# Output projection of a hybrid attention layer on one Trainium2 core: column blocks 2 to 5 with six of 16 pairs of k tiles as 2x2 block products in seven parts

## The chip, the cores and the metric

The kernel runs on one NeuronCore of a Trainium2 chip. The core has a matrix engine (TensorE, PE in the profile, with PEld for its weight loads) and four others that work beside it: VectorE (DVE), ScalarE (ACT), GpSimd (POOL) and SyncE (SP), which here only issues transfers. Each runs its own list of instructions in order and waits on semaphores. PE writes to PSUM, eight banks of 128x512 floats; everything else lies in SBUF.

The metric is the time of one execution on the device, in microseconds (us). A profile is one execution taken by the hardware profiler.

## The reference

One layer with 256 frames and width 4096: an input projection, forgetting attention and an RWKV-7 recurrence side by side, a gate, and then the part that the change is about, the output projection with a residual layer norm:

```python
h = jnp.concatenate([fox_out, rwkv_out], axis=-1) * jax.nn.silu(z.astype(f32))
out = jnp.einsum('bsc,cd->bsd', h.astype(x.dtype), w_out)
x = _layernorm(ALPHA * x.astype(f32) + out.astype(f32), ln_gain, ln_bias, LN_EPS).astype(x.dtype)
```

`h` is 256x4096 and `w_out` 4096x4096, in float32.

## The kernel before

**Products.** Every float32 factor is split in two: `hi`, its rounding to the matrix engine's format (a CAST on ACT, L146), and `lo`, the rest (a TENSOR_TENSOR subtract on DVE, L147). A product of two factors is three matmuls that add up in one PSUM bank: h.hi, l.hi and h.lo, always in this order (L908 to L910). Each is 128x128 times 128x512.

**Tiling.** The 4096 rows of `w_out` are 32 k tiles of 128, taken in 16 pairs `q`; its columns are eight blocks `b` of 512 (`OB`); the 256 frames are two halves `m` of 128. For each block the loop goes over 16 jobs `(b, q)`. A job loads one raw tile of weights (128 x 1024, two k tiles, 512 KB, L226), splits it, and feeds four products (two k tiles, two halves), that is 12 matmuls. Blocks 0 and 1 come first and share the time with the end of the recurrence; their jobs 14 and 15 stand last, in the order (0,14), (0,15), (1,14), (1,15). Then blocks 2 to 7 follow one after the other.

**What sets the order of the weights.** `load` issues raw tiles on SP's queue into four buffers (tag `wr`); `fetch` splits the next one; `weights` keeps three split jobs ahead. There are four buffers for `hi` (tag `wh`) and three for `lo` (tag `wl`), so the `lo` of a job can only be written when PE has done with the `lo` of the job three places before it. A framework's scheduler then writes each engine's list; `issue_after` holds an instruction behind another one of that list.

**Behind each block.** `add` (L923, L924) adds ALPHA times the residual to the bank and takes the statistics for the norm, `gain` (L932) multiplies by the norm's gain, and for the first four blocks L935 and L936 split the second half once more for the end of the kernel. `load_tok(b)` (L887) brings the residual, the gain and two small rows `rr`, from which L899 and L900 make a row for the norm on DVE. The left factor `ht[k]` is a tile of 128 x 2 x 256 (hi and lo of both halves). GpSimd has nothing to do in blocks 2 to 7.

Of the kernel before, what the change touches and what calls it, by code (L numbers as in the profile page):

```python
# [47 lines left out]
HOLD = 46  # L48
W = {"fo": 7, "vs": 2, "np": 4, "gp": 5, "tp": 4, "d1": 8, "d2": 12, "xp": 3, "fs": 4, "fp": 5}
# [38 lines left out]
def layer(ctx: ExitStack, tc: tile.TileContext, xt, xtok, w_main, w_lora, w_first, muv, w_o, up, par, mulora, fbias, lng, lnb, cst, out):  # L88
# [125 lines left out]
    outs = [(b, q) for r in (range(CUT), range(CUT, KT // 2)) for b in range(2) for q in r] + [(b, q) for b in range(2, NB) for q in range(KT // 2)]  # L214
    stream += [(f"wo{b}_{q}", w_o[b][:, 2 * q : 2 * q + 2, :]) for b, q in outs]
# [4 lines left out]
    raws = []  # L220

    def load():
        if stream:
            name, src = stream.pop()
            raw = wpool.tile([P, 1024], F32, tag="wr", name=name, bufs=4)
            nc.sync.dma_start(out=raw, in_=src.rearrange("p k c -> p (k c)"))  # L226
            raws.append((name, raw))

    def fetch():
        while len(raws) < 3 and stream:  # L230
            load()
        if raws:
            name, raw = raws.pop(0)
            if name not in kept:
                ready.append((name, *split(raw, 1024, name)))
                return
            hl = []
            for j in range(4):
                hl.append(xpool.tile([P, OB], F32R, tag=f"x{4 * kept[name] + j}", name=f"{name}_{j}"))
            for j in range(2):  # L240
                r = raw[:, j * OB : (j + 1) * OB]
                nc.scalar.copy(hl[j], r)
                nc.vector.tensor_tensor(hl[2 + j], r, hl[j].bitcast(F32), ALU.subtract)
            ready.append((name, hl[:2], hl[2:]))

    def weights(name):
        while len(ready) < 3 and (stream or raws):
            fetch()
        got, hi, lo = ready.pop(0)
        assert got == name  # L250
        return hi, lo

    def block(n, b):
        if n == 0 and b == 0:
            return acc_0
        acc = [pp.tile([P, 512], F32, tag="pp", name=f"acc{n}_{b}_{m}") for m in range(2)]
        for q in range(KT // 2):
            hi, lo = weights(f"w{n}_{b}_{q}")
# [28 lines left out]
    def issue(out, src):  # L287
        tc.keep_in_program_order(nc.sync.dma_start(out=out, in_=src))
# [16 lines left out]
    lr = const.tile([LORA, 2, 2, S], F32R, name="lr")  # L305
# [596 lines left out]
    def part(t, j):  # L902
        return t[j] if isinstance(t, list) else t[:, j * OB : (j + 1) * OB]

    def project(acc, k, j, m, hi, lo):
        hi, lo = part(hi, j), part(lo, j)
        tt = slice(m * P, (m + 1) * P)
        nc.tensor.matmul(acc, ht[k][:, 0, tt], hi, start=(k == 0), stop=False)  # L908
        nc.tensor.matmul(acc, ht[k][:, 1, tt], hi, start=False, stop=False)  # L909
        nc.tensor.matmul(acc, ht[k][:, 0, tt], lo, start=False, stop=(k == KT - 1))  # L910
# [4 lines left out]
    sums = None  # L915

    def add(m, b):
# [5 lines left out]
        nc.vector.scalar_tensor_tensor(res[m][:, o], res[m][:, o], ALPHA, acc[m], ALU.mult, ALU.add)  # L923
        nc.vector.bn_stats(st[m][:, b, :], res[m][:, o])  # L924
# [5 lines left out]
    def gain(m, b):  # L930
        o = slice(b * OB, (b + 1) * OB)
        nc.vector.tensor_tensor(res[m][:, o], oacc[b][m] if m and b == NB - 1 else res[m][:, o], lgain[b], ALU.mult)  # L932
        if m and b < HALVED:
            gx[b] = [rpool.tile([P, OB], F32R, name=f"g{'hl'[j]}{b}") for j in range(2)]
            nc.scalar.copy(gx[b][0], res[m][:, o])  # L935
            nc.vector.tensor_tensor(gx[b][1], res[m][:, o], gx[b][0].bitcast(F32), ALU.subtract)  # L936

    gx = {}

# [38 lines left out]
    for b, q in outs:  # L978
        if q == 0:
            pool, tag = (ps, "ps") if b == 1 or b and b % 2 == 0 else (pp, "pp")  # L980
            oacc[b] = [pool.tile([P, 512], F32, tag=tag, name=f"oacc{b}_{m}") for m in range(2)]
        acc = oacc[b]
        hi, lo = weights(f"wo{b}_{q}")
        for j in range(2):
# [9 lines left out]
            elif b > 1 and k == (10 if b == 2 else 4):  # L994
                load_tok(b)
            elif (b, k) == (2, 20):
                own = rpool.tile([P, 2, OB], F32, name="own")
# [8 lines left out]
        if q < KT // 2 - 1:  # L1006
            continue
        if b == 0:
# [13 lines left out]
        if b < NB - 1:  # L1022
            with tc.issue_after(latest[0].ins):
                for m in range(2):
                    add(m, b)
                for m in range(2):
                    gain(m, b)
# [75 lines left out]
    folded = [rpool.tile([P, OB], F32R, name=f"f{'hl'[j]}") for j in range(2)]  # L1103
# [97 lines left out]
```

## Time and profile before

| | |
|---|---|
| Time, median of 3 runs | 1914.63 us (1914.19 to 1915.65) |
| The profiled execution: its time, its span | 1915.52 us, 1913.7 us |
| PE busy, DVE busy, ACT busy, POOL busy | 1902.5, 1399.2, 987.5, 261.1 us |
| Granted clock of TensorE, mean | 0.999 |
| Raw tiles of `w_out`: number, size, issue to landing | 128, 512 KB, 4.3 us |
| Stretch 1650 to 1700 us (blocks 2 and 3): PE, DVE, ACT, POOL busy | 50.00, 31.53, 23.78, 0.00 us |

The span is the profiled part of the execution; 1.8 us of the execution's time lie around it. Matmuls overlap in the records (0.39 us each, one begun every 0.23 us), so a busy PE is one that has no gap, not one at its peak. A group of instructions is shown by its line, its engine, output and input, with the number of them, busy time, mean, and then the idle time ahead of them and what ended it.

### The profile page before, as it was taken

To read this page: it belongs to the slowest core of one execution; us is meant where nothing else is said; L and a number is where in the kernel's file an instruction comes from. 1 tells how busy PE (TensorE), PEld (TensorE's weight loads), DVE (VectorE), ACT (ScalarE), POOL (GpSimd) and SP (SyncE) were. 2 spreads that over 40 slices of the span, in tenths; PEclk is the share of its full clock that TensorE was granted. 3 is DMA by queue.
4 is the path that set the end of the run, shared out by engine and by line. 5 is a ranking of instruction groups with operands and counts; after the bars stand their busy time and mean duration, and the time that the engine had idled before them with its cause. 6 is when DMAs were issued, how large, how long until landed. Compare 5 with 4: busy or idle time off the path is not lost.

```text
span 1913.7 us, 28034 instructions
## 1 busy us (share of the span) xinstructions
PE 1902.5 (99%) x9793; PEld 1584.7 (83%) x9793; DVE 1399.2 (73%) x2365; ACT 987.5 (52%) x1539; POOL 261.1 (14%) x465
## 2 busy tenths in 40 slices
PE   9999999999999999999999999999999999999998
PEld 9887888888888888888888888888888878888886
DVE  7578768776877687768776877687778775755555
ACT  6554455456545654465446554645464554444333
POOL 0022002200211021102200220022003201000000
PEclk9999999999999999999999999999999999999999
DMA  9678777776777678767876687668767976766665
GB/s 347 181 209 229 197 203 228 232 222 183 226 229 226 186 225 231 227 188 215 234 227 193 207 249 220 194 208 244 216 195 210 308 247 196 244 210 213 194 215 180
DMA packets 269826, 420.59 MB, mean 220 GB/s; under 512 B 142386, under 2 KB 169668, under 8 KB 269684
## 3 DMA queue, kind: packets, MB, share of 16 engines
q1 hardware_dynamic: 269396, 418.45, 73.0%
q8 instruction: 77, 1.26, 0.3%
q14 instruction: 65, 0.53, 0.1%
q10 hardware_dynamic: 288, 0.34, 0.1%
HBM read 389.07 MB, written 29.64 MB: 219 GB/s over the span
## 4 chain that ended last, share of the span: by engine, by line
PE 97%; DVE 2%; DMA 0%; ACT 0%; issue 0%; SPq 0%; DVEq 0%; ACTq 0%
PE acc L152 24%; PE acc L154 24%; PE acc L153 24%; PE oacc L908 6%; PE oacc L910 6%; PE oacc L909 6%; PE rh L661 1%; PE gp L547 1%; PE up L692 1%; PE sp L702 1%; PE accl L152 1%; PE accl L153 1%; PE accl L154 1%; PE yp L724 0%; PE yp L722 0%; PE fsp L761 0%
## 5 line engine op out<-in xcount | busy, mean ns | idle before, releaser
L776 POOL COPY pT<-lg 32x96 f32<-32x96 f32 x128 | 55.4, 433 | 629.9 <-DVE lg L772 625.1
L584 POOL COPY BKt<-BK 32x192 f32<-32x192 f32 x128 | 73.3, 573 | 62.5 <-DVE BK L581 57.5
L617 DVE TENSOR_REDUCE xc<-prod 128x8 f32<-128x16 f32 (+30 forms) x248 | 72.6, 293 | 6.6
L614 DVE TENSOR_TENSOR prod<-Nb,xc 128x8 f32<-128x8 f32 (+30 forms) x248 | 72.2, 291 | 3.0
L147 DVE TENSOR_TENSOR w_0l<-w,w_0h 128x1024 fp32r<-128x1024 f32 x31 | 38.3, 1234 | 34.8 <-ACT w_0h L146 26.3
L146 ACT CAST w_0h<-w 128x1024 fp32r<-128x1024 f32 x31 | 32.5, 1049 | 58.8 <-DMA w<-in_w_main_dram 36.1
L146 ACT CAST w_8h<-w 128x1024 fp32r<-128x1024 f32 x31 | 32.7, 1054 | 46.8 <-PE acc L153 21.9
L146 ACT CAST w_6h<-w 128x1024 fp32r<-128x1024 f32 x31 | 32.7, 1056 | 46.4 <-PE acc L153 36.4
L147 DVE TENSOR_TENSOR w_11l<-w,w_11h 128x1024 fp32r<-128x1024 f32 x31 | 37.9, 1222 | 21.9 <-PE acc L154 16.2
L147 DVE TENSOR_TENSOR w_9l<-w,w_9h 128x1024 fp32r<-128x1024 f32 x31 | 38.0, 1225 | 20.7 <-issue 9.6
L147 DVE TENSOR_TENSOR w_10l<-w,w_10h 128x1024 fp32r<-128x1024 f32 x31 | 37.9, 1224 | 20.6 <-ACT w_10h L146 7.5
L147 DVE TENSOR_TENSOR w_15l<-w,w_15h 128x1024 fp32r<-128x1024 f32 x31 | 38.1, 1227 | 19.5 <-issue 17.8
L146 ACT CAST w_10h<-w 128x1024 fp32r<-128x1024 f32 x31 | 32.7, 1054 | 35.5 <-DMA w<-in_w_main_dram 22.7
L147 DVE TENSOR_TENSOR w_6l<-w,w_6h 128x1024 fp32r<-128x1024 f32 x31 | 38.9, 1254 | 16.0 <-ACT hry L735 10.3
L146 ACT CAST w_1h<-w 128x1024 fp32r<-128x1024 f32 x31 | 32.7, 1055 | 34.0 <-DMA w<-in_w_main_dram 16.4
L152 PE MATMUL acc<-w_15h,x 128*128 128x512 f32 x124 | 50.2, 405 | 0.0
L152 PE MATMUL acc<-w_9h,x 128*128 128x512 f32 x124 | 50.0, 403 | 0.0
L154 PE MATMUL acc<-w_12l,x 128*128 128x512 f32 x124 | 48.5, 391 | 1.1 <-DVE w_12l L147 1.1
L152 PE MATMUL acc<-w_14h,x 128*128 128x512 f32 x124 | 49.5, 399 | 0.0
L152 PE MATMUL acc<-w_0h,x 128*128 128x512 f32 x124 | 49.1, 396 | 0.0
L152 PE MATMUL acc<-w_2h,x 128*128 128x512 f32 x124 | 49.1, 396 | 0.0
L152 PE MATMUL acc<-w_1h,x 128*128 128x512 f32 x124 | 49.1, 396 | 0.0
(832 smaller groups left out, 6636.2 us busy)
## 6 DMA issues: line engine op xcount, KB each, us to landing
w<-in_w_main_dram SPq DMA_DIRECT2D x496, 512.0 KB, 4.2
wo<-in_w_o_dram SPq DMA_DIRECT2D x128, 512.0 KB, 4.3
bt<-bk SPq DMA_DIRECT2D x88, 128.0 KB, 4.1
Nb<-nd SPq DMA_DIRECT2D x16, 512.0 KB, 4.4
hd<-hl SPq DMA_DIRECT2D x29, 256.0 KB, 2.2
h<-hd SPq DMA_DIRECT2D x29, 256.0 KB, 5.2
wr<-in_w_first_dram SPq DMA_DIRECT2D x15, 384.0 KB, 6.1
lr<-in_w_lora_dram SPq DMA_DIRECT2D x15, 336.0 KB, 6.5
```

The source lines that it names most:

```text
L146: latest[1] = nc.scalar.copy(hi[:, :n], src[:, :n])
L147: latest[0] = nc.vector.tensor_tensor(lo[:, :n], src[:, :n], hi[:, :n].bitcast(F32), ALU.subtract)
L152: nc.tensor.matmul(acc[:, :n], xs[k][:, 0, tt], hi[:, o : o + n], start=(k == 0), stop=False)
L153: nc.tensor.matmul(acc[:, :n], xs[k][:, 1, tt], hi[:, o : o + n], start=False, stop=False)
L154: nc.tensor.matmul(acc[:, :n], xs[k][:, 0, tt], lo[:, o : o + n], start=False, stop=(k == KT - 1))
L584: nc.gpsimd.tensor_copy(BKt[B * b : B * (b + 1), :, :, B * a : B * (a + 1)], BK[B * a : B * (a + 1), :, : NCH - 1, B * b : B * (b + 1)])
L614: first = nc.vector.tensor_tensor(prod[:, :, :, s + 1 :], nb[:, :, s : s + 1, s + 1 :].to_broadcast([P, 2, NJ, w]), xc[:, :, :, s + 1 :], ...
L617: solved = nc.vector.tensor_reduce(xc[:, :, :, s : s + 1], prod[:, :, :, s:], AX.X, ALU.add)
L776: (nc.gpsimd.tensor_copy if b % 2 else nc.scalar.copy)(pT[B * b : B * (b + 1), :, B * a : B * (a + 1)], lg[B * a : B * (a + 1), :, B * b : ...
L908: nc.tensor.matmul(acc, ht[k][:, 0, tt], hi, start=(k == 0), stop=False)
L909: nc.tensor.matmul(acc, ht[k][:, 1, tt], hi, start=False, stop=False)
L910: nc.tensor.matmul(acc, ht[k][:, 0, tt], lo, start=False, stop=(k == KT - 1))
```

## The change

In blocks 2 to 5, taken as the pairs of blocks (2,3) and (4,5), the pairs of k tiles 6 to 11 (`FEW`) are no longer two jobs with eight products but one group with seven (Winograd's form of Strassen's product). With A11, A21 the two halves of `ht[2q]`, A12, A22 those of `ht[2q+1]`, and B11, B21 (block b) and B12, B22 (block b+1) the two k tiles of weights, the sums are

- of weights: t1 = B12 - B11, t3 = B22 - B12 and t4 = B21 - t2 on GpSimd (L277, L278, L282), t2 = B22 - t1 on VectorE (L281);
- of left factors: s1 = A21 + A22, s2 = s1 - A11, s3 = A11 - A21, s4 = A12 - s2, on GpSimd (`combine_left`, six instructions for a q), split by ACT and DVE (`split_left`); s1 is written over A21 and, in block 6, A21 is read back from DRAM.

The products are A11.B11 (bank p1) and A12.B21 in job `e1`, s4.B22 in `e2`, s1.t1 (p5) and s2.t2 (p6) in `e3`, s3.t3 (p7) and A22.t4 in `e4`: 21 matmuls where there were 24. Between the four jobs of a group stand two plain jobs `n` of the same blocks, so a group has 45 matmuls in the order e1 (6), n (12), e2 (3), e3 (6), n (12), e4 (6). Ahead of the six groups stand 6 plain jobs in the first pair of blocks and 4 in the second (`LEAD`), behind them 2 and 4. A raw tile of an `e1` job is held until t4 has read it.

p1, p5, p6 and p7 are banks of their own. `merge` adds them to the residual: eight instructions of 512 columns on DVE for a pair of blocks, and one copy on ACT. What stood behind each block at once (`add`, `gain`, the statistics) now goes through a list `todo`, of which `drain` takes one or two entries for a job. Splitting the second half for the end of the kernel is moved into block 6 (`halves`). The sums of weights and of left factors share two buffers of 128 x 1024 (tag `t`).

The diff, cut to its core:

```diff
+FEW = range(6, 12)
+LEAD = (6, 4)
...
+    plan = [("n", b, q) for r in (range(CUT), range(CUT, KT // 2)) for b in range(2) for q in r]
+    for b, lead in zip((2, 4), LEAD):
+        plain = [[(n, q) for q in range(KT // 2) if q not in FEW] for n in (b, b + 1)]
+        first = [plain[0].pop(0) for _ in range(4)] + [plain[1].pop(0) for _ in range(lead - 4)]
+        plan += [("n", *t) for t in first]
+        for q in FEW:
+            two = [plain[j].pop(0) for j in range(2)]
+            loads += [(b, q), (b + 1, q)] + two
+            plan += [("e1", b, q), ("n", *two[0]), ("e2", b, q), ("e3", b, q), ("n", *two[1]), ("e4", b, q)]
...
+    def combine(kind, b, q):
+        if kind == "e1":
+            t12 = rpool.tile([P, 2 * OB], F32, tag="t", name=f"ta{b}_{q}", bufs=2)
+            t34 = rpool.tile([P, 2 * OB], F32, tag="t", name=f"tb{b}_{q}", bufs=2)
+            nc.gpsimd.tensor_tensor(t12[:, :OB], b12, b11, ALU.subtract)
+            nc.gpsimd.tensor_tensor(t34[:, :OB], b22, b12, ALU.subtract)
+            got = split(raws[one], 2 * OB, one)
+            with tc.issue_after(latest[0].ins):
+                nc.vector.tensor_tensor(t12[:, OB:], b22, t12[:, :OB], ALU.subtract)
+            nc.gpsimd.tensor_tensor(t34[:, OB:], b21, t12[:, OB:], ALU.subtract)
+            return got
+        if kind == "e2":
+            return split(raws.pop(two)[:, OB:], OB, two)
+        t = sums_of[b, q][kind == "e4"]
+        return split(t, 2 * OB, f"{kind}_{b}_{q}")
...
+    def combine_left(q):
+        e, o = ht[2 * q], ht[2 * q + 1]
+        t = lefts[q] = rpool.tile([P, 2 * OB], F32, tag="t", name=f"sf{q}", bufs=2)
+        g(he, e[:, 0, :].bitcast(F32), e[:, 1, :].bitcast(F32), ALU.add)
+        g(ho, o[:, 0, :].bitcast(F32), o[:, 1, :].bitcast(F32), ALU.add)
+        g(s1, he[:, P:], ho[:, P:], ALU.add)
+        g(s2, s1, he[:, :P], ALU.subtract)
+        g(s3, he[:, :P], he[:, P:], ALU.subtract)
+        g(s4, ho[:, :P], s2, ALU.subtract)
...
+    def split_left(q):
+        t = lefts.pop(q)
+        sq[q] = rpool.tile([P, 2, 3 * P], F32R, tag=f"s{q}", name=f"sq{q}")
+        for d, r in ((sq[q], t[:, 2 * S + P :]), (ht[2 * q][:, :, P:], t[:, 2 * S : 2 * S + P])):
+            nc.scalar.copy(d[:, 0, :], r)
+            nc.vector.tensor_tensor(d[:, 1, :], r, d[:, 0, :].bitcast(F32), ALU.subtract)
+        if q + 2 in FEW:
+            combine_left(q + 2)
...
+            if kind == "e1":
+                product(p1, rowsof(2 * q, 0), part(hi, 0), part(lo, 0))
+                product(oacc[b][0], rowsof(2 * q + 1, 0), part(hi, 1), part(lo, 1))
+            elif kind == "e2":
+                product(oacc[b + 1][0], sqof(q, 2), part(hi, 0), part(lo, 0))
+            elif kind == "e3":
+                product(p5, rowsof(2 * q, 1), part(hi, 0), part(lo, 0))
+                product(p6, sqof(q, 0), part(hi, 1), part(lo, 1))
+            else:
+                product(p7, sqof(q, 1), part(hi, 0), part(lo, 0))
+                product(oacc[b][1], rowsof(2 * q + 1, 1), part(hi, 1), part(lo, 1))
```

Until the last jobs of block 1 each engine's list is the same as before, but for the GpSimd sums of q = 6 and 7. Three places show what stands in the lists from there on.

VectorE, before, the middle of block 2 (`wo_4l` is the `lo` of its job 4, `rt` and `rows` are the small rows of `load_tok`):

```order
L147 TENSOR_TENSOR wo_4l<-wo_4_15887,wo_4h 128x1024
L147 TENSOR_TENSOR wo_5l<-wo_5_15905,wo_5h 128x1024
L899 TENSOR_SCALAR rt_15992<-rh_15990,cs 6x512
L900 SCALAR_TENSOR_TENSOR rows<-rr_15987,cs,rt_15992 6x512
L147 TENSOR_TENSOR wo_6l<-wo_6_15923,wo_6h 128x1024
```

VectorE now, in and around the first group (q = 6): `ta_6` holds t1 and t2, `tb_6` t3 and t4; `wo_6l` of 128x512 is the `lo` of `e2`, `e_2_6l` that of `e3` and then of `e4`; `sf_16008` are the left sums of q = 10:

```order
L281 TENSOR_TENSOR ta_6_16030<-wo_6_15985,ta_6_16030 128x512
L1065 TENSOR_TENSOR res_15796<-res_15796,lg_15839 128x512
L1065 TENSOR_TENSOR res_15797<-res_15797,lg_15839 128x512
L149 TENSOR_TENSOR wo_6l<-wo_6_15985,wo_6h 128x512
L149 TENSOR_TENSOR e_2_6l<-ta_6_16030,e_2_6h 128x1024
L1000 TENSOR_TENSOR sq_16103<-sf_16008,sq_16103 128x384
L1000 TENSOR_TENSOR h_14921<-sf_16008,h_14921 128x128
L944 TENSOR_SCALAR rt_16674<-rh_16672,cs 6x512
L945 SCALAR_TENSOR_TENSOR rows<-rr_16669,cs,rt_16674 6x512
L149 TENSOR_TENSOR wo_2l<-wo_2_16065,wo_2h 128x1024
L149 TENSOR_TENSOR e_2_6l<-tb_6_16031,e_2_6h 128x1024
```

Where a plain job had one instruction, a group's jobs have splits, t2, gains of block 1, a split of left sums and the rows of block 4 between them. GpSimd, whose list had ended before, now has in the first group (with the semaphores that each row waits for):

```order
L277 TENSOR_TENSOR ta_6_16030<-wo_6_15985,wo_6_15965 128x512 [waits DMAHW1_49,DMAHW2_49,DVE_49,Activation_49]
L278 TENSOR_TENSOR tb_6_16031<-wo_6_15985 128x512 [waits DVE_49,Pool_49]
L282 TENSOR_TENSOR tb_6_16031<-wo_6_15965,ta_6_16030 128x512
L988 TENSOR_TENSOR sf_16046<-h_14967 128x256 [waits Pool_49]
L989 TENSOR_TENSOR sf_16046<-h_14992 128x256
L992 TENSOR_TENSOR sf_16046<-sf_16046 128x128 [waits Pool_49]
L990 TENSOR_TENSOR sf_16046<-sf_16046 128x128 [waits Pool_49]
L991 TENSOR_TENSOR sf_16046<-sf_16046 128x128 [waits Pool_49]
L993 TENSOR_TENSOR sf_16046<-sf_16046 128x128 [waits Pool_49]
L277 TENSOR_TENSOR ta_7_16139<-wo_7_16097,wo_7_16085 128x512 [waits DMAHW6_49,DMAHW4_49,DVE_49]
```

The two `t` buffers go round as sf8, sf9, sf10, ta_6, tb_6, sf11, ta_7, tb_7: sf10 lies where sf8 lay, ta_6 where sf9 lay, tb_6 where sf10 lay. So t1 of the first group stands behind the split of q = 9, t3 behind the split of q = 10 (the two L1000 rows above), and t1 of the second group behind the `e4` split of the first.

More of the change, by code (lines that the diff above doesn't have):

```diff
@@ L231, in fetch @@
             load()
[L232 to L244, printed above, removed]
@@ L246, in weights @@
-    def weights(name):
-        while len(ready) < 3 and (stream or raws):
+        job = jobs.pop()
+        if job[0][0] == "e":
+            ready.append((job, *combine(*job)))
+            return
+        name = job[0] if len(job) == 1 else f"wo{job[1]}_{job[2]}"
+        raw = raws.pop(name)
+        if name not in kept:
+            ready.append((job, *split(raw, 1024, name)))
+            return
+        hl = []
+        for j in range(4):
+            hl.append(xpool.tile([P, OB], F32R, tag=f"x{4 * kept[name] + j}", name=f"{name}_{j}"))
@@ L248, in weights @@
+    def weights(job):
+        while len(ready) < 3 and jobs:
             fetch()
         got, hi, lo = ready.pop(0)
-        assert got == name
+        assert got == job
         return hi, lo
@@ L912, in layer @@
+    shared = {}
     res = None
@@ new lines, in layer, with finished @@
+    common = {}
+    def finished(b):
+        if b > 5:
+            with tc.issue_after(latest[0].ins):
+                for m in range(2):
+                    add(m, b)
+                for m in range(2):
+                    gain(m, b)
+            return
+        for step in (add, stats, gain):
+            for m in range(2):
+                (behind if step is not add else todo).append(lambda step=step, m=m: step(m, b))
+        if b not in (2, 4):
+            todo.extend(behind)
+            behind.clear()
```

194 lines of the change are left out of this document (155 added, 39 removed).

## The prediction

> **What bounds the kernel now.** I read the busy times first, then the chain that ended last, then the stretches of the output projection.
>
> ```profile
> span 1913.7 us, 28034 instructions
> PE 1902.5 (99%) x9793; PEld 1584.7 (83%) x9793; DVE 1399.2 (73%) x2365; ACT 987.5 (52%) x1539; POOL 261.1 (14%) x465
> ...
> PE 97%; DVE 2%; DMA 0%; ACT 0%; issue 0%; SPq 0%; DVEq 0%; ACTq 0%
> ```
>
> PE is busy for 1902.5 of 1913.7 us and is 97% of the chain: as things stand, a matmul less is its time less. That holds in the changed stretch too:
>
> ```profile
> 1650.00:1700.00 50.00, 50.00 (x222) 41.41 (x221) 31.53 (x35) 23.78 (x26) 0.00 (x0) 1.00 0.76 246
> 1700.00:1750.00 50.00, 50.00 (x223) 41.40 (x222) 27.20 (x28) 20.02 (x20) 0.00 (x0) 1.00 0.67 208
> ```
>
> The columns are the stretch, its length, then busy PE, PEld, DVE, ACT, POOL with counts, and the granted clock. PE never rests; DVE has 18.5 to 22.8 us of each 50 free, POOL all of it. The change spends these to take matmuls away. A matmul's price is the step between starts, since they overlap:
>
> ```profile
> 1700.57 0.39 PE L908 MATMUL oacc<-wo_7h,h 128*128 128x512 f32 x1
> ...
> 1703.29 0.39 PE L908 MATMUL oacc<-wo_8h,h 128*128 128x512 f32 x1
> ```
>
> These rows are 12 matmuls, one job, apart: 2.72 us, 0.2267 each.
>
> **The gain.** Each of the 12 groups has 21 matmuls for 24: 36 fewer, 36 x 0.2267 = **8.2 us** off PE. The Trainium skill, "TensorE: Matmul & The Clock Gate", section on why the gap is 56 and not 53.3 ns, gives 215.7 ns between warm starts of this size; by that the gain would be 7.8 us, an estimate. The trace's step is longer, and the trace decides.
>
> **What DVE and POOL must do for it.** Prices on DVE are steps between starts as well:
>
> ```profile
> 1600.10 1.23 DVE L147 TENSOR_TENSOR wo_6l<-wo,wo_6h 128x1024 fp32r<-128x1024 f32 x1 [3.68 <-PE oacc L910]
> 1601.24 0.70 DVE L468 STREAM_TRANSPOSE hqy<-post 128x512 f32<-128x512 f32 x1
> ...
> 1631.39 0.47 DVE L899 TENSOR_SCALAR rt<-rh,cs 6x512 f32<-6x512 f32 x1
> 1631.90 0.74 DVE L900 SCALAR_TENSOR_TENSOR rows<-rr,cs,rt 6x512 fp32r<-6x512 f32 x1
> 1632.67 1.29 DVE L923 SCALAR_TENSOR_TENSOR res<-res,oacc 128x512 f32<-128x512 f32 x2
> 1633.88 1.28 DVE L924 BATCH_NORM_STATS2 lst<-res 128x6 f32<-128x512 f32 x2
> ```
>
> A `lo` split of 1024 columns takes 1.14 us of DVE's time, two instructions of 512 take 1.21 (0.605 each), an `rt` with its `rows` 1.28. A group has five splits of 1024, one of 512 and t2: 5 x 1.14 + 2 x 0.605 = 6.9 us, where PE needs 45 x 0.2267 = 10.2 us. That alone fits. But POOL's sums run beside it, and the trace shows what happens when both engines work on SBUF operands:
>
> ```profile
> 125.62 1.30 POOL L553 TENSOR_TENSOR vs<-vs,bk 128x512 f32<-128x512 f32 x1
> 125.82 2.19 DVE L147 TENSOR_TENSOR w_6l<-w,w_6h 128x1024 fp32r<-128x1024 f32 x1 [1.43 <-PE acc L154]
> ```
>
> ```profile
> 1454.45 1.39 POOL L551 TENSOR_TENSOR vs<-vs,bk 128x512 f32<-128x512 f32 x1 [12.31 <-DMA vs<-vd]
> ...
> 1454.60 1.52 DVE L510 TENSOR_TENSOR lt<-s,eL 128x256 f32<-128x256 f32 x1
> 1455.92 1.35 POOL L552 TENSOR_TENSOR vs<-vs,muv 128x512 f32<-128x512 f32 x1
> 1456.04 2.95 DVE L515 TENSOR_TENSOR BK<-k,eI 64x256 f32<-64x256 f32 x2
> ...
> 1457.35 1.36 POOL L553 TENSOR_TENSOR vs<-vs,bk 128x512 f32<-128x512 f32 x1
> ```
>
> ```profile
> L510 DVE TENSOR_TENSOR lt<-s,eL x16: 378/420/1546, 91.7 to 1454.6; 128x256 f32<-128x256 f32 x16
> ```
>
> The same `lo` split that takes 1.23 us took 2.19; L510, 0.42 in the median, took 1.52; the two L515 took 2.95 in turn with two sums of POOL. They exclude each other and go in turns, and a POOL sum of 512 that DVE runs into costs DVE 1.1 us (1.52 - 0.42). So a group needs 6.9 + 3 x 1.1 = 10.2 us of DVE and POOL together: **exactly PE's 10.2, with nothing to spare**. Whatever else stands on DVE makes PE wait, beyond the slack that the buffers give.
>
> **That slack.** DVE waits for PE's last `lo` matmuls of three jobs before:
>
> ```profile
> L147 DVE TENSOR_TENSOR wo_14l<-wo,wo_14h 128x1024 fp32r<-128x1024 f32 x8 | 9.8, 1225 | 11.6 <-PE oacc L910 10.5 <-ACT wo_14h L146 1.1
> ```
>
> So at most two jobs lie ready, 5.4 us, and the third matmul of a job needs the `lo`, 0.45 us after its start.
>
> **The start of blocks 2 and 3** is where it is spent. I count from where PE would begin the first e1 (time 0). DVE may begin the `lo` of block 2's first job 8 jobs earlier, at -21.8 us. By its list it then has to pass, up to the left split of q = 10: 9 splits of 1024 (10.3 us), 14 instructions of 512 columns (adds, statistics and gains of blocks 0 and 1, t2, the `lo` of e2: 8.5), five left splits (each 384 + 128 columns, the work of one of 512 in two instructions, 0.67 as an estimate: 3.4), three `rt` and `rows` (3.8): 26 us, with 0.8 for two waits on `lo` buffers, ending at **5**. Beside that POOL makes the left sums of q = 8, 9, 10 and t1. A small sum's price lies between these rows:
>
> ```profile
> L551 POOL TENSOR_TENSOR vs<-vs,bk x8: 1295/1298/1884, 122.0 to 1454.4; 128x512 f32<-128x512 f32 x8
> ...
> L1055 POOL TENSOR_TENSOR za<-mv,zah 128x1 f32<-128x1 f32 x1 | 0.2, 186 | 0.0
> ```
>
> 0.19 us and 2.18 ns for a column; the six of a q have 1024 columns, 3.4 us, of which (as with 1.1 of 1.30) about 2.3 shut DVE out. Three times 2.3 plus 1.1 is 8.0 us. The bounds: DVE loses all 8.0, or, if the eight bank adds and statistics (4.8 us, one operand in SBUF; no run here shows one beside a POOL sum) all run while POOL does, 3.2. I take 5.5, between: DVE's list has them spread and POOL's sums come where they come. The left split of q = 10 then ends at **10.5** (8 to 13). The Trainium skill, "SBUF — State Buffer", "Who interferes with whom", says that a DVE instruction with at most one SBUF input does not contend with GpSimd; by that page alone the better bound, 8, is open, not assured.
>
> t3 waits for this split (it takes its buffer), t4 for t3: 2.6 us of POOL, plus 0.9 as its share of turns with `rows` and a `lo`: 14.0. Only then is the raw tile of e1 free, into whose buffer the weights of the next group's e1 are loaded, and these must be cast:
>
> ```profile
> L146 ACT CAST wo_15h<-wo 128x1024 fp32r<-128x1024 f32 x8 | 8.5, 1057 | 12.1 <-PE oacc L909 10.0 <-DMA wo<-in_w_o_dram 2.1
> ...
> wo<-in_w_o_dram SPq DMA_DIRECT2D x128, 512.0 KB, 4.3
> bt<-bk SPq DMA_DIRECT2D x88, 128.0 KB, 4.1
> ```
>
> 14.0 + 4.3 + 1.06 = 19.4 for the second group's e1, due at 10.2: 9.2 us late, and its `lo` 0.7 later still (1.14 against 0.45). I take **10 us**. Without any turns it is 5 + 2.6 + 4.3 + 1.06 = 13.0, 2.8 late, 3.5 with the `lo`; with all of them 13 + 2.6 + 2.4 + 5.4 = 23.4, about 14.
>
> **The other ten groups** stand at 10.2 against 10.2. Added to them are four more `rt` and `rows` in the first pair and some 19 instructions of 512 columns (merges, adds, statistics, gains) about the second, 5.1 and 11.5 us, most of it beside plain jobs, where DVE needs 1.14 of 2.72 us. Between 0, and 12 if 1.2 us of each group had no cover; I take **3**.
>
> **At no cost.** ACT's casts: 5.9 us of a group's 10.2. The splits of `halves` move to block 6, where DVE is free for 22.8 of 50 us. The six transfers that read A21 back (128 KB, 4.1 us) are issued five jobs, 13.6 us, ahead of use; without that cover they cost 4.1 once. The end of the kernel is untouched.
>
> **The sum:** -8.2 + 10 + 3 = +4.8 us. The profiled execution took 1915.5 us (its span of 1913.7 and 1.8 around), so 1920.3 by it; it is 0.9 over the median of 1914.6, hence **1919.4**.
>
> **Rivals.**
> - *POOL fits into DVE's gaps.* The start costs 3.5, the rest 0.5: 1914.6 - 8.2 + 4.0 = 1910.4, and 1906.4 if all is hidden. It decides if the left split of q = 10 ends by 6 or 7. For it: DVE is free for a third of these stretches. Against: just there the list is full, and the rows show turns, not gaps. 28%.
> - *Half of the turns.* The start costs 5 to 8, the rest 1 to 3: 1912.4 to 1917.4, no change to be told. 25%.
> - *Turns bind in every group*, with 1 us over in each: 1914.6 - 8.2 + 10 + 12 = 1928.4. 8%.
> - *The clock falls in the long wait.* The rows from the program's start show matmuls of 336 columns 0.28 us apart and, later, 0.15:
>
> ```profile
> 5.72 0.48 PE L153 MATMUL accl<-wl0h,x 128*128 128x336 f32 x1
> 6.00 0.48 PE L154 MATMUL accl<-wl0l,x 128*128 128x336 f32 x1
> ...
> 7.67 0.31 PE L153 MATMUL accl<-wl1h,x 128*128 128x336 f32 x1
> 7.82 0.31 PE L154 MATMUL accl<-wl1l,x 128*128 128x336 f32 x1
> ```
>
> From 4.4 to about 6.6 us PE ran at half speed, a loss of 1.1. One such fall on top of the forecast gives 1920.5. The Trainium skill, "TensorE: Matmul & The Clock Gate", "Why this matters for your kernels", warns of PE idle for more than about 3 us; nothing here shows such a gap. 4%.
>
> That the matmuls are not saved is excluded: PE's list has 1500 in the projection for 1536.
>
> **The numbers.** The forecast, slower with a start that costs 8 to 14, has 35%. A measurement of this kernel tells about 0.2%, 3.8 us, from no change. Slower by more: 35 + 8 + 4 = 47%; within: 25%; faster by more: 28%. Cases of both signs hold most: the forecast's own range is 1918 to 1923. The range for 8 in 10 leaves out the turns in every group and the best third of the fitting case: 1908 to 1925.
>
> **What would show it.** The changed profile should have 36 fewer matmuls at 0.227; a wait of PE of several us ahead of the second group's e1, released by ACT or the weights' DMA; `lo` splits of 2.2 us beside POOL's sums; t3 of q = 6 begun right behind the split of q = 10. It is wrong if PE has no wait over 2 us in blocks 2 to 5, or if the waits lie in blocks 4 and 5.

## The result, and the profile after it

The changed kernel takes **1933.8 us** in the median of 4 runs (1932.1 to 1935.5), the kernel before 1915.1 on the same chip: a ratio of **1.0098, 95% interval 1.008 to 1.0115**. It is slower by 18.7 us, where 4.8 were predicted; the direction is right and the time lies outside the range. The first parts of the page, of the changed kernel:

```profile
span 1931.9 us, 28208 instructions
PE 1903.4 (99%) x9757; PEld 1578.9 (82%) x9757; DVE 1466.6 (76%) x2429; ACT 1007.7 (52%) x1577; POOL 358.8 (19%) x537
...
PE 93%; DVE 2%; POOL 2%; DMA 1%; issue 1%; ACT 0%; SPq 0%; DVEq 0%; POOLq 0%; ACTq 0%
```

9757 matmuls are 36 fewer than 9793, as counted, and still PE is busy for longer and only 93% of the chain, where it was 97%: POOL (2%) and a DMA (1%) have come into it. The two stretches shown of before:

```profile
1650.00:1700.00 50.00, 39.61 (x147) 28.61 (x146) 37.61 (x42) 21.39 (x30) 31.44 (x28) 0.93 0.42 147
1700.00:1750.00 50.00, 46.80 (x204) 37.84 (x203) 45.24 (x40) 24.94 (x28) 17.88 (x10) 1.00 0.62 209
```

PE began 222 matmuls in the first stretch before; now it begins 147 and rests for 10 us, and the clock is at 0.93. From the first matmul of block 2 to that of block 6 it is 193.8 us, before 174.1. Less the 8.2 saved it should be 165.9, so 27.9 us are lost, and the stretch is 19.7 us longer. (The two profiled executions differ by 18.2, as the changed one came to block 2 at 1636.6 instead of 1638.0, and the medians by 18.7.) Where, the first matmuls of the groups show (each row has the start in block 2 and that in block 4):

```profile
L960 PE MATMUL p<-wo_6h,h x2: 389/389/389, 1652.9 to 1751.6; 128*128 128x512 f32 x2
L960 PE MATMUL p<-wo_7h,h x2: 389/389/389, 1673.1 to 1761.9; 128*128 128x512 f32 x2
L960 PE MATMUL p<-wo_8h,h x2: 389/389/389, 1688.1 to 1774.1; 128*128 128x512 f32 x2
...
L960 PE MATMUL p<-wo_11h,h x2: 389/389/389, 1723.9 to 1808.1; 128*128 128x512 f32 x2
```

A group of 45 matmuls is due every 10.2 us. The first of block 2 takes 20.2, the second 15.0: 14.8 us lost by two groups. From the third to the last there are 120.0 us where 108.1 are due, and 1.2 more behind that: **13.1 us lost by the other ten**. These take 12.5, 13.1, 10.3 and 11.4 us in block 2 (the last one less the plain jobs behind it) and 10.3, 12.2, 12.3, 10.3, 11.4 and 11.5 in block 4. The longest of what PE waits for in blocks 2 to 5 (us in total, times, longest):

```profile
PE oacc L963 <- DVE wo_12l L149: 3.0, 2, 1.7
PE oacc L963 <- DVE wo_5l L149: 2.9, 2, 1.6
PE oacc L963 <- DVE wo_13l L149: 2.4, 1, 2.4
```

These are the `lo` of **plain jobs** between the jobs of a group, split by DVE, and so are the next two, 2.2 us each for `wo_2l` and `wo_4l`; no wait for an `e1` job stands among them. Two places show why. In a group of block 4 (VectorE, GpSimd, PE; `ta` holds t1 and t2, L277 is t1, L281 t2, L278 t3, L282 t4):

```profile
1773.06 1.77 DVE L281 TENSOR_TENSOR ta<-wo,ta 128x512 f32<-128x512 f32 x1 [1.34 <-POOL ta L277]
...
1775.35 2.30 DVE L149 TENSOR_TENSOR wo_12l<-wo,wo_12h 128x1024 fp32r<-128x1024 f32 x1
```

```profile
1771.73 1.29 POOL L277 TENSOR_TENSOR ta<-wo,wo 128x512 f32<-128x512 f32 x1 [7.43 <-DVE wo_8l L149]
1772.98 1.29 POOL L278 TENSOR_TENSOR tb<-wo 128x512 f32<-128x512 f32 x1
1774.90 1.67 POOL L282 TENSOR_TENSOR tb<-wo,ta 128x512 f32<-128x512 f32 x1 [0.63 <-DVE ta L281]
```

```profile
1777.71 0.50 PE L963 MATMUL oacc<-wo_12l,h 128*128 128x512 f32 x1 [1.67 <-DVE wo_12l L149]
```

DVE waits 1.34 us for t1, then t2 stands for 1.77 us instead of 0.69 because t3 has begun on POOL, then `wo_12l` for 2.30 instead of 1.22 because t4 has: 3.5 us later than without POOL, and PE rests for 1.67. Over all groups:

```profile
L277 POOL TENSOR_TENSOR ta<-wo,wo 128x512 f32<-128x512 f32 x12 | 22.3, 1856 | 71.3 <-DMA wo<-in_w_o_dram 45.5 <-DVE res L1053 18.4 <-DVE wo_8l L149 7.4
L281 DVE TENSOR_TENSOR ta<-wo,ta 128x512 f32<-128x512 f32 x12 | 19.1, 1592 | 14.5 <-POOL ta L277 14.5
```

t2 takes 1.59 us in the mean, and DVE has idled 14.5 us ahead of it, because t1 is late: 2.1 and 2.7 us in the first two groups, 1.2 to 1.3 in eight others, nothing in two. t1 itself mostly waits for its weights to land. Why these are late, the last groups of block 4 show (t1, t4 and the next group's t1 on GpSimd, t2 between them on VectorE, and what SP's queue waits for in that time):

```profile
1794.30 2.14 POOL L277 TENSOR_TENSOR ta<-wo,wo 128x512 f32<-128x512 f32 x1 [5.19 <-DMA wo<-in_w_o_dram]
...
1798.33 2.21 POOL L282 TENSOR_TENSOR tb<-wo,ta 128x512 f32<-128x512 f32 x1 [0.63 <-DVE ta L281]
1805.87 2.07 POOL L277 TENSOR_TENSOR ta<-wo,wo 128x512 f32<-128x512 f32 x1 [5.33 <-DMA wo<-in_w_o_dram]
```

```profile
1796.47 1.77 DVE L281 TENSOR_TENSOR ta<-wo,ta 128x512 f32<-128x512 f32 x1 [1.19 <-POOL ta L277]
```

```profile
SPq L246 <- POOL tb L282: 7.6, 1, 7.6
```

**It is a circle**: t1, t2, t4, the load of the next group's weights, the next t1. t4 ends at 1800.54 and lets go of the raw tile; the loads that SP has held back for 7.6 us go out at 1800.56, and the next t1 begins at 1805.87. Once round is 11.57 us, for a group that PE does in 10.3. The exclusion is part of it: t1, t2 and t4 stand for 2.14, 1.77 and 2.21 us where they take 1.29, 0.69 and 1.29 alone. Without these 2.85 us the circle would be 8.7 us, an estimate, and less than PE's 10.3. As t1 runs while DVE idles, DVE itself meets only two of the three sums in such a group, t3 and t4.

The ten groups fit this. The two in which DVE does not idle ahead of t2 (q = 10 of block 2, q = 6 of block 4) take 10.3 us. Of the eight in which it does, one takes 10.3, three 11.4 or 11.5, and four 12.2 to 13.1: those in which `rt` and `rows`, gains or statistics stand on DVE's list as well.

At the start of blocks 2 and 3 it is another picture (GpSimd's left sums, L988 to L993, then VectorE in the same time):

```profile
1642.51 4.72 POOL L990 TENSOR_TENSOR sf<-sf 128x128 f32<-128x128 f32 x1
1647.30 0.46 POOL L991 TENSOR_TENSOR sf<-sf 128x128 f32<-128x128 f32 x1
```

```profile
1642.09 0.67 DVE L1055 SCALAR_TENSOR_TENSOR res<-res,oacc 128x512 f32<-128x512 f32 x1
1642.68 0.54 DVE L1000 TENSOR_TENSOR sq<-sf,sq 128x384 fp32r<-128x384 f32 x1
1643.15 0.27 DVE L1000 TENSOR_TENSOR h<-sf,h 128x128 fp32r<-128x128 f32 x1
1643.36 1.21 DVE L149 TENSOR_TENSOR wo_0l<-wo,wo_0h 128x1024 fp32r<-128x1024 f32 x1
1644.49 1.28 DVE L1065 TENSOR_TENSOR res<-res,lg 128x512 f32<-128x512 f32 x2
1645.70 1.21 DVE L149 TENSOR_TENSOR wo_1l<-wo,wo_1h 128x1024 fp32r<-128x1024 f32 x1
1648.89 0.56 DVE L1000 TENSOR_TENSOR sq<-sf,sq 128x384 fp32r<-128x384 f32 x1 [1.98 <-ACT sq L999]
```

A sum of 128x128 that takes 0.46 us stands for 4.72 while DVE runs six instructions with two SBUF operands one behind the other (from the first L1000 on; L1055 before them reads a bank); it ends when DVE pauses. DVE is not slowed in these six (1.21 for a `lo`): **GpSimd starves**. And what waits for it is ScalarE:

```profile
1648.34 0.52 ACT L999 CAST sq<-sf 128x384 fp32r<-128x384 f32 x1 [5.24 <-POOL sf L993]
...
1652.90 0.51 ACT L999 CAST sq<-sf 128x384 fp32r<-128x384 f32 x1 [2.90 <-POOL sf L993]
...
1653.52 0.61 ACT L942 CAST rh<-rr 6x512 fp32r<-6x512 f32 x1
1654.04 1.04 ACT L148 CAST wo_4h<-wo 128x1024 fp32r<-128x1024 f32 x1
```

The cast of block 2's next plain job, `wo_4h`, and that of the small rows stand behind it on ACT's list; `rt` on DVE waits for the latter, `wo_4l` stands behind `rt`, and PE waits 0.67 us for the one and 2.21 for the other. The other long wait of this group, 2.22 us for `wo_2l`, begins with the same sums: t1 stands behind them on GpSimd's list, one of them takes 2.98 us, t1 begins at 1658.84, and DVE idles 2.13 us ahead of t2 (1660.15), with eight more instructions between that and `wo_2l`.

Then the clock. PE's steps from that wait on:

```profile
1658.08 0.50 PE L963 MATMUL oacc<-wo_4l,h 128*128 128x512 f32 x1 [2.21 <-DVE wo_4l L149]
...
1659.18 0.63 PE L960 MATMUL oacc<-wo_4h,h 128*128 128x512 f32 x1
1659.61 0.63 PE L961 MATMUL oacc<-wo_4h,h 128*128 128x512 f32 x1
```

Steps of 0.43 us instead of 0.2267, until 1662.2; the same from 1669.2 to 1672.6 behind the 2.22 us for `wo_2l`, where the granted clock is 0.51. Some eight matmuls each, about 1.6 us each.

### The profile page after: what moved, and what is told of

Read it like the earlier page. It is cut to its first block, busy times and chain, and to the rows that moved or that the text cites. A ratio compares the mean times of both kernels' runs of the same rounds, so it can differ in the third digit from the quotient of the medians.

```text
span 1931.9 us, 28208 instructions
## 1 busy us (share of the span) xinstructions
PE 1903.4 (99%) x9757; PEld 1578.9 (82%) x9757; DVE 1466.6 (76%) x2429; ACT 1007.7 (52%) x1577; POOL 358.8 (19%) x537
## 4 chain that ended last, share of the span: by engine, by line
PE 93%; DVE 2%; POOL 2%; DMA 1%; issue 1%; ACT 0%; SPq 0%; DVEq 0%; POOLq 0%; ACTq 0%
PE acc L154 24%; PE acc L156 23%; PE acc L155 23%; PE oacc L963 5%; PE oacc L960 4%; PE oacc L961 4%; PE rh L706 1%; PE gp L592 1%; PE up L737 1%; PE sp L747 1%; PE accl L154 1%; PE accl L155 1%; PE accl L156 1%; DMA wo<-in_w_o_dram 1%; PE yp L769 0%
## 5 line engine op out<-in xcount | busy, mean ns | idle before, releaser
L149 DVE TENSOR_TENSOR w_6l<-w,w_6h 128x1024 fp32r<-128x1024 f32 x31 | 38.9, 1253 | 16.1 <-ACT hry L780 10.3
L518 POOL COPY hr<-hr 32x16 f32<-32x16 f32 x64 | 45.4, 709 | 26.8 <-DVE hr L515 24.4
L149 DVE TENSOR_TENSOR w_7l<-w,w_7h 128x1024 fp32r<-128x1024 f32 x31 | 37.9, 1221 | 15.1 <-PE acc L156 13.1
```

The source lines that it names most:

```text
L149: latest[0] = nc.vector.tensor_tensor(lo[:, :n], src[:, :n], hi[:, :n].bitcast(F32), ALU.subtract)
```

## The experiments

The runs are called e1 to e12; the jobs of a group are written `e1` to `e4`. In the expectations "port" is the exclusion of DVE and POOL, "start" the first two groups, and 1906.8 the time before less the 8.2 us of the matmuls. The expectations count 10 us for the first group and 18 for the eleven behind it. Each result stands beside the time of the kernel before on the same chip (1914.6 to 1915.3). First, what all of them did to the groups, from the first matmuls of the `e1` jobs: the time of the first two groups over the 20.4 us due, and that from the third group of block 2 to the last of block 4 over the time due (108.1; 105.4 and 113.6 where `LEAD` differs). These are good to 0.1. In each row 0.2 and 0.9 us of them are no waits: a group takes 10.30 us even without any (e6 below), not the 10.2 that count as due.

| kernel | median, us | ratio, 95% interval | first two, us over | the rest, us over |
|---|---|---|---|---|
| the change | 1933.8 | 1.0098 (1.008 to 1.0115) | 14.8 | 11.9 |
| e1, weight sums on VectorE | 1922.8 | 1.0044 (1.0029 to 1.0059) | 12.7 | 4.2 |
| e2, weight sums as copies | 1919.6 | 1.0023 (1.0014 to 1.0033) | 12.0 | 1.1 |
| e3, t2 and t4 behind the plain `lo` | 1926.0 | 1.0059 (1.0044 to 1.0074) | 13.6 | 6.4 |
| e4, left sums on VectorE | 1931.1 | 1.0087 (1.0072 to 1.0102) | 9.6 | 15.2 |
| e5, all sums on VectorE | 1914.2 | 0.9994 (0.9985 to 1.0003) | 4.8 | 2.6 |
| e6, all sums as copies | 1912.7 | 0.9988 (0.9979 to 0.9997) | 4.8 | 1.7 |
| e7, e5 with a lead of 7 | 1914.4 | 0.9995 (0.9985 to 1.0005) | 4.1 | 4.2 |
| e8, e7 with t2 and t4 behind | 1914.0 | 0.9994 (0.9985 to 1.0004) | 4.1 | 2.4 |
| e9, five raw buffers | 1928.5 | 1.0073 (1.0057 to 1.0088) | 14.8 | 7.4 |
| e10, e5 with left sums early | 1912.7 | 0.9986 (0.9977 to 0.9995) | 0.9 | 4.9 |
| e11, e10 with t2 and t4 behind | 1914.6 | 0.9998 (0.9989 to 1.0006) | 1.2 | 7.9 |
| e12, e10 with leads of 6 | 1911.0 | 0.9981 (0.9972 to 0.999) | 0.7 | 4.5 |

**e1.** Who makes the weight sums.

```diff
-            nc.gpsimd.tensor_tensor(t12[:, :OB], b12, b11, ALU.subtract)
+            nc.vector.tensor_tensor(t12[:, :OB], b12, b11, ALU.subtract)
```

(t3 and t4 likewise.)

> The three weight sums t1, t3, t4 of each group on VectorE in place of GpSimd; the left sums stay on GpSimd. DVE's list then has 8.7 us a group (five splits of 1.14, one of 512 columns and four sums at 0.605), under PE's 10.2, and meets GpSimd only at the start of blocks 2 and 3. Port theory (what costs the groups is that sums of GpSimd and of DVE shut each other out): the ten later groups' 18 us go almost entirely, the start keeps its 10: 1933.8 - 16 = 1918, 1913 to 1923, and the sums t2 fall from 1.59 to 0.6 us. Buffer theory (t4 holds e1's raw tile, so the next group's weights land late): t4 ends 1 to 2 us sooner, worth 5 at most: 1927 to 1933. Order theory (n1's lo is late because sums stand ahead of it on DVE): two more sums of 0.6 stand there, slower than the change: 1938 to 1945.

1922.8: the upper end of what the port theory gave, and neither of the others. The rest falls from 11.9 to 4.2, the start only from 14.8 to 12.7.

**e2.** GpSimd's weight sums as copies.

```diff
-            nc.gpsimd.tensor_tensor(t12[:, :OB], b12, b11, ALU.subtract)
+            nc.gpsimd.tensor_copy(t12[:, :OB], b12)
```

> t1, t3 and t4 stay on GpSimd but are copies of 128x512 (one operand in SBUF) instead of differences, so the weight sums are left out of the result; t4 still waits for t2. Port theory (two operands in SBUF on both sides are what excludes): DVE's t2 and lo run at 0.6 and 1.23 us beside them, and the time is that of the sums on VectorE or better, 1911 to 1920. If GpSimd's length and its place in the chain t1, t2, t4 is what counts and not the exclusion: copies take about as long as sums, and the time stays within 5 of 1933.8. Buffer theory: raw tiles come free at t2 instead of t4, 2 us sooner a group: 1922 to 1928 with t2 still near 1.6 us.

1919.6, the rest at 1.1: the time that the port theory gave, but not for its reason. VectorE and GpSimd in a group of this kernel:

```profile
1772.50 1.09 DVE L281 TENSOR_TENSOR ta<-wo,ta 128x512 f32<-128x512 f32 x1
...
1763.95 1.63 DVE L149 TENSOR_TENSOR wo_12l<-wo,wo_12h 128x1024 fp32r<-128x1024 f32 x1
```

```profile
1771.50 1.55 POOL L278 COPY tb<-wo 128x512 f32<-128x512 f32 x1 [1.14 <-DVE e_8l L149]
```

A copy shuts DVE out as well, only for less: t2 takes 1.09 instead of 0.69, `wo_12l` 1.63 instead of 1.22. That is 0.40 us for a copy (0.61 long when alone, below) where a sum (1.29) costs 1.08. At these two lengths, with one operand or two, the cost is what GpSimd's instruction takes alone, less 0.21 us. The Trainium skill, "SBUF — State Buffer", "Who interferes with whom", has it so: a DVE instruction with two SBUF inputs contends with a GpSimd instruction that reads SBUF. This run agrees; the expectation did not.

**e3.** The order on DVE and POOL.

```diff
-            with tc.issue_after(latest[0].ins):
-                nc.vector.tensor_tensor(t12[:, OB:], b22, t12[:, :OB], ALU.subtract)
-            nc.gpsimd.tensor_tensor(t34[:, OB:], b21, t12[:, OB:], ALU.subtract)
+            def rest():
+                with tc.issue_after(latest[0].ins):
+                    nc.vector.tensor_tensor(t12[:, OB:], b22, t12[:, :OB], ALU.subtract)
+                nc.gpsimd.tensor_tensor(t34[:, OB:], b21, t12[:, OB:], ALU.subtract)
+
+            pending.append(rest)
...
             ready.append((job, *split(raw, 1024, name)))
+            if pending:
+                pending.pop()()
```

> t2 on DVE and t4 on GpSimd are issued behind the lo split of the plain job that follows e1, nothing else changed. Order theory (t2, waiting for t1 and shut out by t3, stands ahead of that lo): eight waits of PE of 1.3 to 2.4 us for that lo go, 1918 to 1924. Port theory: the exclusion only moves to another split, t2 then delays the lo of e2 and t4 that of e3: 1928 to 1936. Buffer theory: t4 ends later and holds e1's raw tile longer: 1936 to 1945.

1926.0, between the two: neither alone. Its group of t2:

```profile
L286 DVE TENSOR_TENSOR ta<-wo,ta 128x512 f32<-128x512 f32 x12 | 9.3, 771 | 2.1 <-POOL ta L280 2.1
```

DVE's idle time ahead of t2 falls from 14.5 to 2.1 us and t2 from 1.59 to 0.77; the rest falls by 5.5.

**e4.** The left sums alone on VectorE.

```diff
-        g = nc.gpsimd.tensor_tensor
+        g = nc.vector.tensor_tensor
```

> The left sums (six small sums for each of the six pairs of k tiles) on VectorE in place of GpSimd; the weight sums stay on GpSimd. Start as the prediction had it (DVE's list is full there): 3 sums in front for four q, about 1.6 us a q, make the start worse than with GpSimd only if the exclusion costs less than 1.6 us a q: by the prediction's 5.5 for three q the two nearly cancel, 1930 to 1936. Port theory with GpSimd starved (a sum of 0.46 us took 4.72 while DVE ran on): the left sums end sooner, t3 of the first group comes 3 to 5 us sooner: 1925 to 1930. The groups from the third on are not touched by either.

1931.1, as if the two had cancelled, but they did not: the start loses 5.2 us less, the rest 3.3 more, which the expectation had ruled out. Part of the 3.3 is the clock: in the third group it falls behind a wait of 1.99 us (at 1688.30), with seven steps of 0.43 us. In the first group it falls once, behind two shorter waits (1.36 and 0.53 us).

**e5.** e1 and e4 together: no sum on GpSimd.

> Weight sums and left sums all on VectorE, none on GpSimd. Without any loss the time would be 1915.0 - 8.2 = 1906.8. Port theory for the start (GpSimd's small left sums starve beside a busy DVE, ACT's casts of them wait, and the casts of weights stand behind these): with none on GpSimd the start's 12 us fall to about 5, the rest stays at the 4 us of the run with the weight sums alone on VectorE: 1916, 1911 to 1919. List theory (the prediction's: DVE simply has too much to do there): the left sums add about 1.6 us a pair to a full list, five pairs: 8 us more than the 1922.8 of that run, 1927 to 1932.

1914.2, inside the port theory's range and 13 us below the list theory's: the start falls from 14.8 to 4.8, though DVE has more to do there.

**e6.** All of GpSimd's sums as copies (e2, and the same for the left sums).

> Every sum of GpSimd, of weights and of left factors, is a copy with one operand; DVE's instructions and the order are those of the change (the sums are left out of the result). Port theory: DVE meets no exclusion anywhere, GpSimd's copies end in their own time, and the 12 us that are left with the weight copies alone fall to 0 to 4: 1907 to 1911, faster than before. List theory: the start keeps its 12, as DVE's list is the same: 1917 to 1921.

1912.7, below the kernel before, but no kernel to use, as it leaves the sums out; 1.7 us above what the port theory gave, and more than 4 below the list theory. The start is at 4.8 again. The shorter instructions are still starved where DVE does not pause, and are not where DVE reads one operand from PSUM (GpSimd, then VectorE's two L1053 with a bank in `oacc`):

```profile
1642.10 4.17 POOL L993 COPY sf<-sf 128x128 f32<-128x128 f32 x1
...
1733.15 0.61 POOL L282 COPY tb<-ta 128x512 f32<-128x512 f32 x1 [1.74 <-DVE ta L281]
```

```profile
1733.01 1.27 DVE L1053 TENSOR_TENSOR res<-res,oacc 128x512 f32<-128x512 f32 x2
```

This kernel also has groups with no wait at all, so it shows what a group costs by itself:

```profile
1756.68 0.39 PE L960 MATMUL p<-wo_8h,h 128*128 128x512 f32 x1
...
1760.76 0.40 PE L960 MATMUL oacc<-wo_8h,sq 128*128 128x512 f32 x1
1761.00 0.39 PE L961 MATMUL oacc<-wo_8h,sq 128*128 128x512 f32 x1
...
1766.98 0.39 PE L960 MATMUL p<-wo_9h,h 128*128 128x512 f32 x1
```

10.30 us for 45 matmuls, not 10.20: steps around the products of left sums (`sq`) are 0.23 to 0.24. For 12 groups that is 1.2 us of the 8.2.

**e7.** e5 with `LEAD = (7, 4)`.

> All sums on VectorE, and seven plain jobs ahead of block 2's first group instead of six (the tail of the pair is one shorter). What DVE is behind at the start then has 2.7 us more, of which its own split takes 1.1. List theory and port theory both: 1.5 to 3 us less than all sums on VectorE with six, if that run still loses at the start; no change if it doesn't. A candidate: 1911 to 1916.

1914.4, no change, and so a miss: e5 still lost 4.8 us at the start, for which both theories gave 1.5 to 3 us less. The first two groups gain 0.7 and the rest loses 1.6. The stretch of 30 us that holds the start (columns as above), in the change, in e7 and in e10, below:

```profile
1636.00:1666.00 30.00, 26.43 (x105) 20.01 (x103) 23.40 (x34) 11.80 (x19) 22.18 (x21) 0.94 0.46 158
```

```profile
1636.00:1666.00 30.00, 26.74 (x116) 21.15 (x115) 29.70 (x64) 14.25 (x25) 0.00 (x0) 1.00 0.58 183
```

```profile
1636.00:1666.00 30.00, 30.00 (x131) 24.14 (x129) 28.27 (x41) 17.89 (x27) 0.00 (x0) 1.00 0.65 214
```

In the change DVE works 23.40 of the 30 us. Until 1647, 6 us ahead of the first `e1`, its list is full (15.04 of the 15.80 us from 1631.2); from there **it waits** (12.79 of 19.00 us). With all sums on it, it is full (29.70), and one more job is no help.

**e8.** e7 with the order of e3 (t2 and t4 on VectorE).

> As the run with all sums on VectorE and seven jobs ahead, with t2 and t4 behind the lo of the plain job that follows e1. Order theory (t2 ahead of that lo is what makes PE wait, whoever makes the sums): the waits for that lo in blocks 4 and 5 go, 2 to 4 us less than without it. Port theory (order counted only because GpSimd's turns stretched what stood ahead): within 1.5 us of it.

1914.0, 0.4 less: the port theory's answer. Without GpSimd's turns the order is worth nothing that can be told.

**e9.** A fifth buffer for raw weights, sums on GpSimd.

```diff
+        if n % 5 == 4:
+            raw = rpool.tile([P, 1024], F32, tag="wo", name=name)
...
-        while len(raws) < 3 and stream:
+        while len(raws) < (3 if rpool is None else 4) and stream:
```

> Sums on GpSimd and the order as in the change; a fifth buffer for raw weights (from the output's pool, every fifth load) and four instead of three tiles loaded ahead. To make room, rt is written over rh and the zero matrices of the end share a tile; the work is the same. Buffer theory (t4 holds e1's raw tile, so t1 of the next group waits for its weights: GpSimd idle 45.5 us for these DMAs ahead of t1): t1 begins up to 4 us sooner, t2 and the lo behind it too: 1918 to 1926. Port theory: an earlier t1 meets the same exclusion, and lo is late for t2, t3 and t4's turns: 1930 to 1935.

1928.5, between the two ranges. The idle time ahead of t2 goes (14.5 to 2.8 us) and the rest falls by 4.5, much as in e3; the start doesn't change:

```profile
L287 DVE TENSOR_TENSOR ta<-wo,ta 128x512 f32<-128x512 f32 x12 | 16.9, 1412 | 2.8 <-POOL ta L283 2.8
```

t2 itself still takes 1.41 us: the buffers are why t1 is late, the exclusion is why t2 and `lo` are long, and each costs. Of the 7.4 that are left, about 1.5 are a fall of the clock behind a wait of 2.43 us (at 1703), which the change does not have. The last two groups of block 4 take 10.30 us each, where the change took 11.4 and 11.5, though DVE now meets all three sums in them (two are shown, the third is at the `lo` of `e2`, 1.78 us):

```profile
1800.45 2.31 DVE L149 TENSOR_TENSOR wo_11l<-wo,wo_11h 128x1024 fp32r<-128x1024 f32 x1
...
1802.69 1.78 DVE L287 TENSOR_TENSOR ta<-wo,ta 128x512 f32<-128x512 f32 x1
```

So with its weights in time a group does fit, full as DVE's list is; **the circle through the raw tiles is what these two lost by**.

**e10.** e5, with the left sums of the first four pairs made in block 1's last jobs, and those of the last two within the groups. `rt` moves to ACT, and empty entries in `todo` spread what is left.

```diff
+        ha, hb, oa, ob = (t[:, n * P : (n + 1) * P] for n in range(4))
...
+        g(ob, hb, ob, ALU.add)
+        g(hb, ha, hb, ALU.subtract)
+        g(ha, ob, ha, ALU.subtract)
+        g(oa, oa, ha, ALU.subtract)
...
+            for q in FEW[:4:2]:
+                t = rpool.tile([P, 2 * OB], F32, tag="t", name=f"sf{q}", bufs=2)
+                for j in range(2):
+                    combine_left(q + j, t[:, j * OB : (j + 1) * OB])
```

> All sums on VectorE; the left sums of the first four pairs are made in place in 512 columns each, in block 1's last jobs where VectorE has pauses, those of the last two within the groups; rt is made by ACT. Port and list together (with no exclusion left, what stays of the loss is VectorE's full list at the start): about 10 us of VectorE's work leave the first two groups, the waits there go, and with 1 us for the slower steps of the left products the time is 1906.8 + 1 + 0 to 4: 1910, 1908 to 1913, faster than before. If the start's loss had another cause (ACT's queue, the weights' DMA): 1913 to 1916 as with all sums on VectorE.

1912.7, in the range and **faster than before** by 0.05 to 0.23%. The start is at 0.9 us; PE has no wait in its first 30 us (the third of the three rows above) while DVE still works 28.27. What is left, 4.9, lies mostly in the first groups of block 4.

**e11.** e10 with the order of e3.

> As the run with the left sums early, with t2 and t4 behind the lo of the plain job that follows e1. Order theory without exclusion: up to 2 us less, since that lo has only t1 and t3 ahead; otherwise within 1 us: 1908 to 1912.

1914.6: 2.6 above the range, a miss for both. PE waits 2.5 us for `wo_0l` in block 4's first group, once, and the clock falls behind that.

**e12.** e10 with `LEAD = (6, 6)`.

> As the run with the left sums early, with six plain jobs ahead of block 4's first group instead of four. What is left there of waits (1.0 and 1.5 us for the lo of plain jobs in blocks 4 and 5) is by the list theory VectorE's merging of blocks 2 and 3, 17 instructions of 512 columns in the first jobs of block 4: with 5.4 us more the waits go, 1910.2, 1909 to 1912. By the buffer theory (t1 on VectorE waits 2.7 and 1.2 us for its weights to land, with the lo of the plain job queued behind it) the same waits come two jobs later: 1912 to 1914.

1911.0, the best of all. Its waits:

```profile
PE oacc L962 <- DVE wo_2l L149: 1.8, 1, 1.8
PE oacc L962 <- DVE wo_4l L149: 0.6, 1, 0.6
```

The time is that of the list theory, the waits are those of the buffer theory (nearly the same, two jobs later). The rest is at 4.5, nearly all of it in two things: 0.9 of slower steps, and 3.5 at four places where PE waits for the `lo` of a plain job, with steps of 1.00, 2.23, 0.43 and 0.28 us and one of 0.34 behind each. The view shows only two of these, and less than they cost, as a matmul's record (0.39 us) is longer than its step. By the ratios e12 is 1 us better than e10 with intervals that overlap: the two are not told apart.

## Why the prediction was wrong

**The gain** was right in number (36 matmuls) and 1.2 us too high in time: a group takes 10.30 us without a wait, where 45 x 0.2267 is 10.20.

**The step that failed is "The other ten groups ... I take 3"**: they cost 13.1, over the bound of 12, 1.0 of it the slower steps. The sum that stands ahead of it is right. A sum of GpSimd that DVE runs into costs 1.08 us (t2 1.77, `wo_12l` 2.30, against 0.69 and 1.22), 1.1 was taken; and in e9 groups that meet three sums do run in PE's time. What failed is to take a group in which the work just fits for one that loses next to nothing. The work is in a chain: t4 holds a raw tile, the next weights wait for t4, t1 for the weights, t2 for t1. The prediction has this chain for the weights of the second group only, but it goes round in the others too. From one t1 to the next are 11.4 us or more in seven of the eight steps within a block and 10.9 in one, for PE's 10.3, and DVE idles in it. The second part of the step, that `rt`, `rows`, gains and statistics are covered by plain jobs, failed in the four groups that take 12.2 to 13.1. The rival "turns bind in every group", with 1 us over in each, had about this size and was given 8%, but three of the ten groups lost only 0.1. The experiments bear out both parts of the circle: without the long sums of GpSimd the rest falls from 11.9 to 4.2 (e1) and 1.1 (e2); with them, but with the idle time ahead of t2 taken away by the order (e3) or by a buffer (e9), to 6.4 and 7.4.

**The start** was given 10 us. At the second group's `e1`, where the prediction measures it, it is 10.0 (20.2 for 10.2): the size is right, and by luck. The second group then loses 4.8 more, for which the sum has no term. The work on DVE was counted well: 26 us up to the left split of q = 10, and DVE is busy for 26.2 of the 33.06 us from its first `lo` (1631.39) to the end of that split (1664.45), 11.5 us behind the first `e1`, for which 10.5 were forecast. But "go in turns", with 5.5 us lost by DVE, fails: the instructions that GpSimd slows there (two `rt`, one `rows`, one L1000) are some 1.5 us longer in sum, while GpSimd's small sums wait out whole runs of DVE instructions. In place of the turns stand 6.8 us in which DVE is idle, where 0.8 were counted. The raw tile held by t4 is not what the second `e1` waits for: its cast begins at 1669.80, 1.0 us behind the end of t4, and a load takes 4.3. PE waits for `lo` of plain jobs, behind casts on ACT and a t1 that wait for the left sums. Without GpSimd's sums (e5), or with copies in their place (e6), the start loses 4.8: 10.0 of the 14.8 come with the sums, the clock's 3.2 among these; e10 shows that most of the other 4.8 go when VectorE's work there is spread.

**The clock**, a rival at 4%, fell twice, 1.6 us each, both in the first group: 3.2 of its 10.0. The Trainium skill, "TensorE: Matmul & The Clock Gate", "Why this matters for your kernels", gives idle gaps above about 3 us as what to avoid. Here it fell behind gaps of 2.21 and 2.22 us, and of 1.99 in e4; and not behind one of 2.44 at 1705 us, though it did behind one of 2.43 in e9. The bound of 3 us does not hold here, and length alone does not decide.

**What was to show it**: the 36 matmuls, `lo` splits of 2.2 us beside POOL's sums (2.30), and t3 of q = 6 right behind the split of q = 10 (1664.60 behind 1664.17) are there. The wait ahead of the second `e1` is not, and 6.7 of the 27.9 us lie in blocks 4 and 5 (5.5 to the last group's `e1`, 1.2 behind it), which the prediction named as a sign that it is wrong.

**Left open:** why GpSimd gets in behind one VectorE instruction (t4 above) and not behind six in a row; what else than its length decides whether a wait lowers the clock; and why the seven jobs ahead in e7 gained nothing.

## What to carry to other kernels

Engines that hand work to and fro are not to be priced by adding up their busy times alone: look for the circle that goes through them, through the buffer that its last link lets go of and the load that waits for it, time it once round, and compare that with the time of the bound engine. Then look at which later instruction stands behind the waiting one. GpSimd is no free engine beside a VectorE that reads two SBUF operands at a stretch: where VectorE had the time, the sums cost 7 us on it instead of 27 (e5 and the change, over 1906.8). A saving on the bound engine is worth making only if the work that it causes lies in the pauses of the others: the same 36 matmuls fewer are 18.7 us slower with the sums on GpSimd and 2.4 us faster with them on VectorE and early (e10).

## What the runs showed of the hardware

- A GpSimd instruction of 0.29 to 0.46 us (128x128) stood for 4.17, 4.72 and, in e1, 6.00 us beside VectorE instructions with two SBUF operands that followed one another; in e1 it ended while one with a single SBUF tensor (`rt`) ran. Beside one with an operand in PSUM a copy of 512 columns took its 0.61.
- A VectorE instruction that meets a GpSimd sum of 128x512 (1.29 us alone) loses 1.08 us, one that meets a copy (0.61) 0.40.
- The clock of TensorE went to about half (0.51 granted, steps of 0.43 us) for 3.0 to 3.4 us behind single waits of 1.99 to 2.43 us (the change, e3, e4, e9), and for 5.7 behind the longest (4.86 us, e9); behind one of 2.44 us it stayed at 1.00.
- With left factors from `sq`, matmul steps were up to 0.24 us instead of 0.2267.
